# Keeping a convolution's output in DRAM instead of adding it up again from its two halves

## The chip, the cores and the metric

The kernel runs on one core of one Trainium2 chip, as one program in one launch. The metric is the device time of an execution in microseconds (us). Where a profile is shown, it comes from one profiled execution; its span runs from the first to the last instruction. The engines are called by the profile's names: PE is TensorE (PEld its weight loads), DVE is VectorE, ACT is ScalarE, POOL is GpSimd, and SP is the sequencer that issues most DMAs.

## The reference

One inference step of a small two-layer decoder trunk, all in float32: 1024 prompt tokens and 8 sequences of 4 sample tokens, 1056 columns together, model width 1024. The first layer is a gated linear recurrence (RG-LRU) of width 1536, the second one is HGRN2. Only the first is touched here:

```python
def _causal_conv(xb, w, b, buf):
    T = xb.shape[1]
    xp = jnp.concatenate([buf.astype(xb.dtype), xb], axis=1)
    out = b
    for k in range(CONV_W):
        out = out + w[k] * xp[:, k:k + T]
    return out, xp[:, -(CONV_W - 1):]

def _rg_lru(xc, w_r, b_r, w_i, b_i, lam, h0):
    ...
    r = jax.nn.sigmoid(jnp.einsum('btni,nij->btnj', xh, w_r.astype(jnp.float32)).reshape(Bsz, T, W) + b_r)
    ig = jax.nn.sigmoid(jnp.einsum('btni,nij->btnj', xh, w_i.astype(jnp.float32)).reshape(Bsz, T, W) + b_i)
    log_a = -LRU_C * jax.nn.softplus(-lam.astype(jnp.float32)) * r
    a = jnp.exp(log_a)
    bterm = jnp.sqrt(-jnp.expm1(2.0 * log_a)) * (ig * xf)
    bterm = bterm.at[:, 0].add(a[:, 0] * h0.astype(jnp.float32))
    _, h = lax.associative_scan(_lru_combine, (a, bterm), axis=1)
    return h, h[:, -1]

def _lru_layer(x, g_norm, w_in, conv_w, conv_b, w_r, b_r, w_i, b_i, lam, w_out, h0, buf):
    xn = _rmsnorm(x, g_norm)
    u = xn @ w_in
    xb, gate = u[..., :W_LRU], u[..., W_LRU:]
    xc, new_buf = _causal_conv(xb, conv_w, conv_b, buf)
    h, h_last = _rg_lru(xc, w_r, b_r, w_i, b_i, lam, h0)
    y = (h * jax.nn.silu(gate.astype(jnp.float32))).astype(x.dtype)
    return x + y @ w_out, h_last.astype(x.dtype), new_buf.astype(x.dtype)
```

The convolution's output `xc` (in `_rg_lru` also `xf` and `xh`) is used three times: in the two gate products, and as the factor of `ig` in the recurrence's input.

## The kernel before

**Layout.** Features lie on the 128 partitions, tokens along the columns. The 1056 columns are worked in three chunks of 352 (`CH`, `NCH`). The 1536 features of the recurrence are 12 tiles `m` of 128, in four groups `g` of three tiles `j`.

**Products.** A float32 product is made of three matmuls (`mm3`, L245 to L249): both operands are split into a high and a low part of a shorter type, and high x high, high x low and low x high are summed in PSUM. `weights` (L378) loads a weight tile in pieces of 512 columns into a ring of three raw buffers, casts the high part on ACT and subtracts the low part on POOL or DVE into rings of four pieces each. `product` (L401) then runs 8 blocks of 128 rows, 24 matmuls of 352 columns, into one of four PSUM banks.

**The convolution** (`conv`, L474). For a tile and a chunk, the product is copied into `xb`, ACT starts `t` with the last tap (L508), and DVE adds three taps (L511). `t` is a buffer of a ring of three (`ts`), cut out of the tile `k`. Then a DMA copies 32 of its rows to `ST` (L514), ACT writes the high part of `t` (L516) and DVE the low part (L517) into `X`, the operands of the gate products.

**The recurrence** (`lru`, L549). For a group and a chunk: gate products from `X` (L573) and from `ST` (L579), Tanh on ACT, DMAs that put 32 rows of each result in place (`R<-td`, L585), then for each tile `j` the recurrence's input: POOL adds the two parts of `X` into a buffer `x` (L594, a ring of two, `xrs`, also cut out of `k`), DVE multiplies it with the gate (L595), and further DVE instructions and a scan (L615) follow.

**The order of the work.** Every operation is first recorded by `Flow.add` with its engine, an estimated duration, what it reads and writes, and a priority. `Flow.plan` (L104) lays the operations out on five engines (SP's queue is one of them, a DMA counts as an SP operation with a transfer time behind it), `Flow.back` derives new priorities from the end backwards, eight times, and for the first layer `Flow.search` (L171) tries 3000 random changes of the priorities in its first 60 us. The resulting order is what each engine gets. The estimate for POOL instructions marked `both` also holds back DVE instructions marked so (L123). The order of the big products on PE is fixed in the code (`main=True`): for the first layer, groups of gate and convolution tiles with `lru(g)` and the output products `out(g)` woven in (L908 to L930). Each engine runs its list in order; SP runs its DMA issues in order too, and each waits for its own semaphores.

At the start, 48 matmuls on a constant tile (L739) are recorded with the lowest priority and fill what PE has free.

The helpers that record one operation:

```python
        def dma(dst, src, r=(), w=(), prio=5, kb=180, q=Q):
            fl.add("SP" if q is Q else "ACT", 0.45, lambda: q.dma_start(dst, src), r, w, prio, kb * (1.0 if r else 0.75))
...
        def pool(n, emit, r, w, prio=5):
            fl.add("POOL", 0.1 + 0.00245 * n, emit, r, w, prio, both=True)
...
        ks = [(KR[:, chunk(i)], ("k", i)) for i in range(KB)]
        ts, xrs = cycle(ks[:3]), cycle(ks[3:])
```

Of the kernel before, what the change touches and what calls it, by code (L numbers as in the profile page):

```python
# [14 lines left out]
F32 = mybir.dt.float32  # L15
# [4 lines left out]
ALU = mybir.AluOpType  # L20
# [21 lines left out]
TOK = SEQ + NB * NS  # L42
CH = 352
# [3 lines left out]
ML = WL // 128  # L47
# [168 lines left out]
def tile_trunk(ctx: ExitStack, tc: tile.TileContext, xT, prm, hc, w0, wg, wo0, w1, wo1, s_in,  # L216
               yT, h_out, c_out, sp_out, ss_out):
    nc = tc.nc
    V, S, G, T, Q = nc.vector, nc.scalar, nc.gpsimd, nc.tensor, nc.sync
# [15 lines left out]
    def pc(name, j, n=1):  # L235
        a = PRM[name][0] + j
        return P[:, a:a + n]
# [4 lines left out]
    def chunk(c):  # L242
        return slice(c * CH, (c + 1) * CH)
# [26 lines left out]
    x1a = [nc.dram_tensor(f"x1a_{m}", (128, TOK), F32, kind="Internal").ap() for m in range(KD)]  # L270
    x1d = [nc.dram_tensor(f"x1_{m}", (128, TOK), F32, kind="Internal").ap() for m in range(KD)]

    xn = nc.dram_tensor("xn", (KD, 128, TOK), F32, kind="Internal").ap()

    KR = chunks.tile([128, KB * CH], F32, tag="k", bufs=1, name="k")
# [27 lines left out]
    with ExitStack() as l0:  # L303
# [12 lines left out]
        def dma(dst, src, r=(), w=(), prio=5, kb=180, q=Q):  # L316
            fl.add("SP" if q is Q else "ACT", 0.45, lambda: q.dma_start(dst, src), r, w, prio, kb * (1.0 if r else 0.75))
# [6 lines left out]
        def act(n, emit, r, w, prio=5, more=0.0):  # L324
            fl.add("ACT", 0.25 + 0.0007 * n + more, emit, r, w, prio)

        def dve(n, emit, r, w, prio=5, both=False):
            fl.add("DVE", 0.13 + 0.0011 * n, emit, r, w, prio, both=both)

        def pool(n, emit, r, w, prio=5):  # L330
            fl.add("POOL", 0.1 + 0.00245 * n, emit, r, w, prio, both=True)
# [41 lines left out]
        def xpart(j, i, c):  # L373

            b = 6 * c + 2 * j + i
            return X[:, b * CH:(b + 1) * CH], ("X", b)
# [97 lines left out]
        def conv(g, head=False):  # L474

            items = []
            for j in range(3):
                m = 3 * g + j
                mine = {}

                def evac(c, ps, pk, by=None, j=j, m=m, mine=mine):
                    n = CH if c < 2 else 1024 - 2 * CH
                    if c == 0:
                        mine[0] = next(xbs)
                        pool(3, lambda xb=mine[0][0]: G.memset(xb[:, :3], 0.0), (), (mine[0][1],), 2)
                    elif head:
                        mine[c] = next(xbs)
                        pool(3, lambda xb=mine[c][0]: G.tensor_copy(xb[:, :3], tails[:, 4 * j:4 * j + 3]), (("tail", j),), (mine[c][1],), 0)
                    xb, xk = mine[c]
                    t, tk = next(ts)  # L490
                    if by:
                        dve(n, lambda: V.tensor_tensor(xb[:, 3:3 + n], ps[:, :n], by[0], op=ALU.mult), (pk, by[1]), (xk,), 0)
                        pool(3, lambda: G.tensor_copy(tails[:, 4 * j:4 * j + 3], xb[:, n:n + 3]), (xk,), (("tail", j),), 1)
                    else:
                        act(n, lambda: S.copy(xb[:, 3:3 + n], ps[:, :n]), (pk,), (xk,), 0)
                    if c < 2 and not by:
                        nx, nk = mine[c + 1] = (tails[:, 4 * j:], ("tail", j)) if head else next(xbs)
                        act(3, lambda: S.copy(nx[:, :3], ps[:, CH - 3:CH]), (pk,), (nk,), 0)
                    parts = [(xb[:, :3 + n], t[:, :n], lambda ap, i: ap[:, i:i + n], n)]
                    if c == 2:  # L500
                        xs = xb[:, 323:379].rearrange("p (b j) -> p b j", j=7)
                        pool(24, lambda: G.tensor_copy(xs[:, :, :3], cs[:, m]), (("hct",),), (xk,), 1)
                        act(32, lambda: S.copy(xs[:, :, 3:], ps[:, n:CH].rearrange("p (b j) -> p b j", j=4)), (pk,), (xk,), 0)
                        pool(3, lambda: G.tensor_copy(cst[:, m, 0, :], xb[:, 320:323]), (xk,), (("cst", m),), 4)
                        pool(24, lambda: G.tensor_copy(cst[:, m, 1:, :], xs[:, :, 4:7]), (xk,), (("cst", m, 1),), 4)
                        parts.append((xs, t[:, n:].rearrange("p (b j) -> p b j", j=4), lambda ap, i: ap[:, :, i:i + 4], 32))
                    for src, dst, sh, u in parts:
                        act(u, lambda src=src, dst=dst, sh=sh: S.activation(dst, sh(src, 3), AF.Identity, bias=pc("cb", m),  # L508
                                                                         scale=pc("cw", 36 + m)), (xk, ("P",)), (tk,), 1, 0.1)
                        for k in range(3):  # L510
                            dve(u, lambda src=src, dst=dst, sh=sh, k=k: V.scalar_tensor_tensor(  # L511
                                dst, sh(src, k), pc("cw", 12 * k + m), dst, op0=ALU.mult, op1=ALU.add), (xk, tk), (tk,), 1, True)
                    w = slice(32 * j, 32 * j + 32)
                    dma(ST[w, chunk(c)], t[w], (tk,), (("ST", j, c),), 1, 45)  # L514
                    (a, ak), (b, bk) = xpart(j, 0, c), xpart(j, 1, c)
                    act(CH, lambda: S.copy(a, t), (tk,), (ak,), 1)  # L516
                    dve(CH, lambda: V.tensor_tensor(b, t, a.bitcast(F32), op=ALU.subtract), (tk, ak), (bk,), 1, True)  # L517

                items.append((w0[m], evac))
            return items  # L520

# [27 lines left out]
        def lru(g):  # L549
# [11 lines left out]
            for c in range(NCH):  # L561
# [5 lines left out]
                for i, hb in ((0, hbr), (1, hbi)):  # L567
                    for j in range(3):
                        m = 3 * g + j
# [16 lines left out]
                for j in range(3):  # L586
                    m = 3 * g + j
                    act(CH, lambda j=j, m=m, ta=ta, ab=ab: S.activation(ab[:, j], ta[:, j], AF.Exp, bias=cn[:, m:m + 1], scale=cn[:, m:m + 1]),
                        (tak[j], ("sm",)), (("a", s, j),), 3, 0.15)
                    act(CH, lambda j=j, m=m, ta=ta: S.activation(ta[:, j], ta[:, j], AF.Tanh, bias=cp[:, m:m + 1], scale=cp[:, m:m + 1]),  # L590
                        (tak[j], ("sm",)), (tak[j],), 3, 0.15)
                    x, xk = next(xrs)
                    (a, ak), (b, bk) = xpart(j, 0, c), xpart(j, 1, c)
                    pool(CH, lambda x=x, a=a, b=b: G.tensor_tensor(x, a.bitcast(F32), b.bitcast(F32), op=ALU.add), (ak, bk), (xk,), 3)  # L594
                    dve(CH, lambda x=x, j=j, ti=ti: V.scalar_tensor_tensor(ti[:, j], ti[:, j], 1.0, x, op0=ALU.add, op1=ALU.mult),  # L595
                        (xk, tik[j]), (tik[j],), 3, True)

# [4 lines left out]
                for j in range(3):  # L602
                    m = 3 * g + j
# [302 lines left out]
        ysum = nc.dram_tensor("ysum", (3, 128, 8, HT), F32, kind="Internal").ap()  # L906
        x1b = [nc.dram_tensor(f"x1b_{m}", (128, TOK), F32, kind="Internal").ap() for m in range(KD)]
        lru(0)  # L908
        split_y(0)
        run(project0(gate(1)))  # L910
        run(project0(conv(1)))
        gates, rest = project0(gate(2)), out(0, xT, x1a)
        run(islice(gates, 6))
        lru(1)
        run(gates)
        run(project0(conv(2)))
        lru(2)
        run(rest)
        split_y(1)
# [19 lines left out]
    with ExitStack() as l1:  # L939
# [59 lines left out]
        def ykeys(m, a, n):  # L999

            return [("Y", m, i) for i, (u, v) in enumerate(zip(CUTS, CUTS[1:])) if u < a + n and v > a]
# [805 lines left out]
        for a, n in OUT:  # L1807
# [3 lines left out]
            acc, ak = next(accs)  # L1811
            tot, tk = next(hg)
            own = 4 if final else PS
            for m in range(KD):
# [12 lines left out]
                x, xk = x2[m][:, q], ykeys(Y2 + m, a, n)  # L1827
# [84 lines left out]
```

## Time and profile before

| | |
|---|---|
| median of the runs | 1056.82 us |
| lowest run | 1049.51 us |
| the profiled execution | 1050.79 us |
| its span | 1049.0 us |
| granted clock of TensorE, mean | 0.996 |
| HBM read / written | 81.60 / 33.05 MB |

Busy times in the page are shares of the span on each engine. Matmuls overlap: the next one starts before the last one has ended, so the time from start to start tells more than the length of one. "Idle before" of a group is the time that its engine stood still just ahead of it, with the instruction or DMA that ended the wait.

### The profile page before, as it was taken

Reading aid. Unit: us, or ns where it says so; the run is one execution under the profiler, and the core shown is the slowest. Engines: PE = TensorE matmul, PEld = TensorE weight load, DVE = VectorE, ACT = ScalarE, POOL = GpSimd, SP = SyncE. Lnnn points to the kernel's source line nnn. Section 1 sums busy time; section 2 is a strip of 40 time slices with the busy share of each in tenths; the row PEclk is TensorE's granted clock in tenths of the full one; section 3 lists DMA queues with packets and bytes.
Section 4 is the critical chain, followed back from the end, with each engine's and each line's share of the span. In section 5 each row is a group of like instructions: output and inputs, shape, how many; then the busy total and the mean of one; then the engine's idle time right before and its main releaser. Section 6 shows DMA issues by size and latency. Waiting matters only on the chain.

```text
span 1049.0 us, 26022 instructions
## 1 busy us (share of the span) xinstructions
PE 1029.1 (98%) x10174; PEld 1006.9 (96%) x10174; DVE 762.1 (73%) x1474; ACT 677.1 (65%) x1534; POOL 501.2 (48%) x526
## 2 busy tenths in 40 slices
PE   9999999999999999999999999999899999999995
PEld 9999999999999999999999999999899999999994
DVE  8999996788898689355687655555657567898648
ACT  6578656877775765334378685857577675785453
POOL 3425443544534355644655555555455453145454
PEclk9999999999999999999999999999999999999998
DMA  9101112123751586445676575655567662764644
GB/s 309 58 23 52 54 51 71 48 71 96 224 188 52 165 267 188 151 121 183 208 193 146 120 173 113 151 117 151 112 148 178 150 169 76 251 151 113 128 91 165
DMA packets 90763, 143.69 MB, mean 137 GB/s; under 512 B 11152, under 2 KB 56592, under 8 KB 90640
## 3 DMA queue, kind: packets, MB, share of 16 engines
q1 hardware_dynamic: 74656, 112.46, 34.0%
q0 software_dynamic: 13680, 26.81, 15.1%
q10 hardware_dynamic: 2304, 2.77, 0.8%
q8 instruction: 79, 1.29, 0.5%
q14 instruction: 44, 0.36, 0.1%
HBM read 81.60 MB, written 33.05 MB: 109 GB/s over the span
## 4 chain that ended last, share of the span: by engine, by line
PE 88%; DVE 8%; DMA 3%; issue 1%; ACT 0%; SPq 0%; ACTq 0%; DVEq 0%
PE mm L247 25%; PE mm L248 24%; PE mm L249 24%; PE hg L1063 2%; PE hg L1281 1%; PE hg L579 1%; PE hg L1174 1%; PE hg L1283 1%; PE hg L247 1%; PE hg L248 1%; PE hg L249 1%; DVE R L1045 1%; PE hg L1235 1%; DMA a<-in_w_dram 1%; DMA wraw<-in_wo_dram 1%; DVE R L445 1%
## 5 line engine op out<-in xcount | busy, mean ns | idle before, releaser
L247 PE MATMUL mm<-xh,whi 128*128 128x352 f32 (+1 forms) x1147 | 353.9, 309 | 5.0 <-DVE sg L1543 4.2
L248 PE MATMUL mm<-xl,whi 128*128 128x352 f32 (+1 forms) x1147 | 348.5, 304 | 0.0
L249 PE MATMUL mm<-xh,wlo 128*128 128x352 f32 (+1 forms) x1147 | 348.3, 304 | 0.0
L247 PEld LDWEIGHTS mm<-xh,whi 128*128 128x128 f32 x1147 | 215.5, 188 | 7.9 <-DVE sg L1543 4.8
L248 PEld LDWEIGHTS mm<-xl,whi 128*128 128x128 f32 x1147 | 215.6, 188 | 1.4
L249 PEld LDWEIGHTS mm<-xh,wlo 128*128 128x128 f32 x1147 | 215.6, 188 | 0.0
L335 POOL TENSOR_TENSOR wlo<-wraw,whi 128x512 fp32r<-128x512 f32 (+1 forms) x62 | 90.2, 1463 | 82.6 <-ACT whi L390 73.5
L247 PE MATMUL mm<-t,whi 128*128 128x264 f32 x408 | 118.3, 290 | 0.0
L249 PE MATMUL mm<-t,wlo 128*128 128x264 f32 x408 | 115.9, 284 | 0.7 <-POOL wlo L335 0.7
L248 PE MATMUL mm<-t,whi 128*128 128x264 f32 x408 | 115.7, 284 | 0.0
L511 DVE SCALAR_TENSOR_TENSOR k<-xb,prm_sb,k 128x352 f32<-128x352 f32 (+2 forms) x144 | 90.1, 637 | 10.9 <-ACT k L508 7.7
L247 PEld LDWEIGHTS mm<-t,whi 128*128 128x128 f32 x408 | 76.8, 188 | 0.9
L249 PEld LDWEIGHTS mm<-t,wlo 128*128 128x128 f32 x408 | 76.6, 188 | 0.9 <-POOL wlo L335 0.9
L248 PEld LDWEIGHTS mm<-t,whi 128*128 128x128 f32 x408 | 76.9, 188 | 0.1
L322 POOL DMA_DIRECT2D wlo<-wraw x52 | 45.4, 874 | 65.0 <-ACT wlo L321 45.9
L1543 DVE TENSOR_TENSOR k<-mm,k 128x264 f32<-128x264 f32 x72 | 30.8, 430 | 59.6 <-PE mm L249 56.4
L594 POOL TENSOR_TENSOR k<-X 128x352 f32<-128x352 f32 x36 | 43.8, 1226 | 48.0 <-DVE R L595 38.4
L322 POOL DMA_DIRECT2D wlo<-R x32 | 29.3, 923 | 44.7 <-ACT wlo L321 39.6
L247 PE MATMUL mm<-yh,whi 128*128 128x352 f32 x153 | 49.9, 326 | 0.0
L390 ACT CAST whi<-wraw 128x512 fp32r<-128x512 f32 (+1 forms) x63 | 36.3, 591 | 20.5 <-DMA wraw<-in_w_dram 10.1
L249 PE MATMUL mm<-yh,wlo 128*128 128x352 f32 x153 | 49.4, 323 | 0.0
L248 PE MATMUL mm<-yl,whi 128*128 128x352 f32 x153 | 49.4, 323 | 0.0
(423 smaller groups left out, 2688.7 us busy)
## 6 DMA issues: line engine op xcount, KB each, us to landing
wraw<-in_w_dram SPq DMA_DIRECT2D x88, 256.0 KB, 3.4
wlo<-wraw POOLq DMA_DIRECT2D x49, 256.0 KB, 4.2
wlo<-R POOLq DMA_DIRECT2D x30, 256.0 KB, 4.2
wraw<-in_wo_dram SPq DMA_DIRECT2D x37, 192.0 KB, 2.8
ysum<-sg SPq DMA_DIRECT2D x9, 528.0 KB, 5.2
si<-in_s_in_dram SPq DMA_DIRECT2D x8, 512.0 KB, 4.1
R<-in_w_dram SPq DMA_DIRECT2D x16, 256.0 KB, 3.6
out_ss_out_dram<-si SPq DMA_DIRECT2D x8, 512.0 KB, 2.9
```

What stands on the lines that cost most here:

```text
L247: T.matmul(out, wh, xh, start=first, stop=False, skip_group_check=chained)
L248: T.matmul(out, wh, xl, start=False, stop=False, skip_group_check=chained)
L249: T.matmul(out, wl, xh, start=False, stop=last, skip_group_check=chained)
L322: fl.add("POOL", 0.93, lambda: G.dma_start(dst.bitcast(F32), src, accum_op=ALU.add), (*r, *w), w, prio, n / 2)
L335: emit = lambda: e.tensor_tensor(b, x, a.bitcast(F32), op=ALU.subtract)
L390: act(m, lambda hi=hi, raw=raw, m=m: S.copy(hi[:, :m], raw[:, :m]), rk, (hk,), prio)
L445: (pool if e is G else dve)(CH, lambda: e.tensor_tensor(a[:, :CH], a[:, :CH], sq, op=ALU.add), (sk, ak), (ak,), 2)
L511: dve(u, lambda src=src, dst=dst, sh=sh, k=k: V.scalar_tensor_tensor(dst, sh(src, k), pc("cw", 12 * k + m), dst, op0=ALU.mult, op1=ALU.add ...
L579: fl.add("PE", 0.62, lambda ps=ps, i=i, c=c: T.matmul(ps[:96, :CH], gs[:, i, :], ST[:96, chunk(c)], start=True, stop=True), (("gs",), *((" ...
L594: pool(CH, lambda x=x, a=a, b=b: G.tensor_tensor(x, a.bitcast(F32), b.bitcast(F32), op=ALU.add), (ak, bk), (xk,), 3)
L1063: T.matmul(ps[32 * j:32 * j + 32, n * w:n * w + w], B[:, o:o + 32], q(slice(o, o + 32)), start=True, stop=True, tile_position=(0, 32 * j))
L1543: dve(QT, lambda: V.tensor_tensor(o[0], z[0], u[0], op=ALU.add), (z[1], u[1]), (o[1],), 0)
```

## The change

`conv` additionally stores the whole of `t` (128 rows, 352 columns) to a new DRAM tensor `tx`, right behind the small DMA to `ST`. `lru` loads this tile back into `x` with a DMA, where POOL added the two parts of `X`. Both DMAs are issued by SP. The value that the recurrence multiplies is then `t` itself. The same happens for all 12 tiles and three chunks.

```diff
@@ -270,6 +270,7 @@
     x1d = [nc.dram_tensor(f"x1_{m}", (128, TOK), F32, kind="Internal").ap() for m in range(KD)]
 
+    tx = nc.dram_tensor("tx", (ML, 128, TOK), F32, kind="Internal").ap()
     xn = nc.dram_tensor("xn", (KD, 128, TOK), F32, kind="Internal").ap()
@@ -512,6 +513,7 @@
                     w = slice(32 * j, 32 * j + 32)
                     dma(ST[w, chunk(c)], t[w], (tk,), (("ST", j, c),), 1, 45)
+                    dma(tx[m][:, chunk(c)], t, (tk,), (("tx", m, c),), 1)
                     (a, ak), (b, bk) = xpart(j, 0, c), xpart(j, 1, c)
@@ -590,8 +592,7 @@
                     x, xk = next(xrs)
-                    (a, ak), (b, bk) = xpart(j, 0, c), xpart(j, 1, c)
-                    pool(CH, lambda x=x, a=a, b=b: G.tensor_tensor(x, a.bitcast(F32), b.bitcast(F32), op=ALU.add), (ak, bk), (xk,), 3)
+                    dma(x, tx[m][:, chunk(c)], (("tx", m, c),), (xk,), 3)
                     dve(CH, lambda x=x, j=j, ti=ti: V.scalar_tensor_tensor(ti[:, j], ti[:, j], 1.0, x, op0=ALU.add, op1=ALU.mult),
                         (xk, tik[j]), (tik[j],), 3, True)
```

## The prediction

> **What bounds the kernel now.** I read the page's head first, then where the busy time of each engine lies by stage, then who TensorE waited for, and last the matmuls one by one. The page:
>
> ```profile
> span 1049.0 us, 26022 instructions
> PE 1029.1 (98%) x10174; PEld 1006.9 (96%) x10174; DVE 762.1 (73%) x1474; ACT 677.1 (65%) x1534; POOL 501.2 (48%) x526
> PE 88%; DVE 8%; DMA 3%; issue 1%; ACT 0%; SPq 0%; ACTq 0%; DVEq 0%
> ```
>
> TensorE is busy for 98% of the span and makes 88% of the chain that ended last; GpSimd, which the change relieves, is not in that chain's list at all. A share of busy time is an average, so the next view cuts the span into stages (columns: length, then busy time and instructions of each engine, granted clock, DMA share, GB/s):
>
> ```profile
> 0.00:18.00 18.00, 16.96 (x118) 16.96 (x119) 13.32 (x33) 12.58 (x26) 5.72 (x13) 1.00 0.91 314
> 18.00:44.00 26.00, 25.90 (x161) 24.95 (x161) 25.20 (x53) 16.43 (x35) 12.90 (x13) 1.00 0.44 138
> 44.00:534.00 490.00, 490.00 (x3101) 482.80 (x3102) 382.14 (x674) 304.60 (x594) 230.37 (x256) 1.00 0.40 123
> 534.00:944.00 410.00, 404.01 (x6078) 394.26 (x6067) 267.88 (x567) 293.77 (x751) 202.56 (x193) 1.00 0.62 150
> 944.00:1049.00 105.00, 92.22 (x744) 87.92 (x742) 73.51 (x152) 49.77 (x130) 49.59 (x53) 0.96 0.49 124
> ```
>
> The third row is the first layer after its start: 490.00 us of TensorE in 490.00 us. All of TensorE's idle time, 1049.0 - 1029.1 = 20 us, lies in the other rows, and nearly all of it behind 534 us, in the second layer and the tail, which the diff doesn't touch. The waits of TensorE, whole kernel (us in all, times, longest):
>
> ```profile
> PE mm L247 <- DVE sg L1543: 4.2, 3, 2.9
> PE hg L740 <- DVE ones L259: 1.0, 1, 1.0
> PE mm L1226 <- issue: 0.8, 1, 0.8
> PE mm L247 <- DVE vst L1190: 0.8, 1, 0.8
> PE mm L249 <- POOL wlo L335: 0.7, 1, 0.7
> PE mm L1226 <- DVE R L1697: 0.5, 1, 0.5
> PE hg L1149 <- DVE sg L1045: 0.4, 1, 0.4
> ```
>
> No row names a line of the first layer's recurrence (L549 to L625) as what TensorE waited for. Matmuls overlap, so "busy" could still hide bubbles; their starts tell:
>
> ```profile
> 120.05 0.32 PE L247 MATMUL mm<-xh,whi 128*128 128x352 f32 x1
> 120.21 0.32 PE L248 MATMUL mm<-xl,whi 128*128 128x352 f32 x1
> 120.37 0.32 PE L249 MATMUL mm<-xh,wlo 128*128 128x352 f32 x1
> ```
>
> One starts every 0.16 us, although each lasts 0.32; 490.00 / 3101 = 0.158 us for the stage as a whole is the same pace. The stage is a closed row of matmuls at a granted clock of 1.00. The change removes no matmul, so this stage can't become shorter than 490 us.
>
> [...]
>
> **The change part by part.** The removed and the neighbouring work, from the lines' own answers (count, then minimum/median/maximum in ns, first and last start in us), and from the groups:
>
> ```profile
> L594 POOL TENSOR_TENSOR k<-X x36: 934/1171/2000, 85.8 to 394.5; 128x352 f32<-128x352 f32 x36
> L594 POOL TENSOR_TENSOR k<-X 128x352 f32<-128x352 f32 x36 | 43.8, 1226 | 48.0 <-DVE R L595 38.4 <-DVE X L517 7.3 <-DVE nr L452 1.9
> L595 DVE SCALAR_TENSOR_TENSOR R<-R,k x36: 509/524/1622, 87.8 to 395.5; 128x352 f32<-128x352 f32 x36
> L595 DVE SCALAR_TENSOR_TENSOR R<-R,k 128x352 f32<-128x352 f32 x36 | 28.9, 820 | 10.1 <-DMA R<-td 8.0 <-POOL k L594 2.1
> L317 SPq DMA_DIRECT2D ST<-k x36: 507/512/1707, 48.6 to 355.8; - x36
> ```
>
> (1) Removed: 36 additions on GpSimd, 36 x 1.226 = 43.8 us of its 230.37 us in the stage. GpSimd had 490.00 - 230.37 = 260 us to spare there; TensorE waited for none of the 36. Worth 0 us on the path. Vector waited 2.1 us for them in all, also beside TensorE.
>
> (2) Relief of VectorE: L595 takes 509 ns at best and 820 ns on average, so something stretches it by 36 x 0.31 = 11 us. GpSimd runs beside it, and with 36 GpSimd instructions gone part of that goes. VectorE has 382.14 of 490.00 us, so the 11 us (at most the 43.8 us that GpSimd gives up) fall into its own slack of 108 us: 0 us on the path.
>
> [...]
>
> (3) Added: 36 stores and 36 loads of 128 x 352 x 4 bytes = 176 KB. No row has exactly these, but stores and loads of the same tiles and size to and from DRAM are there (KB, us from issue to landing):
>
> ```profile
> ST<-k SPq DMA_DIRECT2D x36, 44.0 KB, 1.8
> x1a<-k SPq DMA_DIRECT2D x9, 176.0 KB, 3.2
> k<-x1a SPq DMA_DIRECT2D x9, 176.0 KB, 3.8
> wraw<-in_w_dram SPq DMA_DIRECT2D x88, 256.0 KB, 3.4
> ```
>
> A tile thus takes 3.2 + 3.8 = 7.0 us through DRAM, where the addition took 1.2. It has far longer: the small store of the same `t` (ST<-k) runs from 48.6 to 355.8 us and the additions from 85.8 to 394.5, so the first value is wanted 37 us, and the last 39 us, after it exists. The latency costs 0 us. Were a load late all the same, L595 would wait, and behind it on VectorE the taps and the copies that empty TensorE's banks. Traffic: 72 x 180,224 bytes = 13.0 MB; at the 314 GB/s of the first row of stages (DMA share 0.91) that is 41 us of full DMA, spread over about 350 us in a stage with a share of 0.40. It becomes about 0.5. The crowded place is the end of the layer:
>
> ```profile
> 346.00:396.00 50.00, 50.00 (x304) 48.54 (x303) 36.96 (x61) 38.86 (x66) 26.29 (x21) 1.00 0.75 229
> ```
>
> There some 9 loads and a few stores join, 12 x 0.18 MB / 314 GB/s = 7 us into 50 us that have 12 us free. It fits, by little.
>
> (4) SP's queue: 72 issues more, at the 0.51 us of the small store's row 37 us of sequencer time. All of SP's issues stand in order, so what counts is who is held behind a waiting one. The store follows the small store of the same tile and waits for the same VectorE instruction, so it adds no wait. The load waits for its buffer `x` (two of them), that is for the L595 of two tiles before, and behind it stand weight loads. SP's queue already does such waiting:
>
> ```profile
> SPq L317 <- DVE k L511: 65.2, 22, 14.9
> SPq L317 <- POOL wlo L335: 64.7, 32, 10.0
> ```
>
> (Between 44 and 434 us.) It stood up to 14.9 us behind a convolution tile without TensorE noticing. The cover is the ring of four weight pieces: a piece of 512 columns feeds 4 blocks x 3 chunks x 3 matmuls x 0.16 = 5.8 us, so the two pieces ahead feed 11.5 us. The nearest row for the new wait is the addition's wait for the same buffer, today on GpSimd's queue:
>
> ```profile
> POOL k L594 <- DVE R L595: 38.4, 14, 8.1
> ```
>
> So the ends are 0 and 38.4 us, for holds of at most 8.1. As 8.1 is under the cover of 11.5, I take 0.
>
> (5) `t` is held until the larger store has landed, 3.2 instead of 1.8 us, plus 0.5 us of issue: 1.9 us longer in a ring of three. ScalarE's next write of `t` would queue behind it, then the release of the product's PSUM bank. A product takes 24 x 0.16 = 3.8 us and there are four banks, so 1.9 us stay covered.
>
> (6) The order of the whole first layer is planned again with the new costs, and the random search over its first 60 us draws differently. Where this shows is the start, in which idle matmuls fill the holes between real ones:
>
> ```profile
> 10.31 0.41 PE L247 MATMUL mm<-xh,whi 128*128 128x352 f32 x1
> 11.34 2.17 PE L740 MATMUL hg<-ones 128*128 128x128 f32 x18
> 15.46 1.27 PE L740 MATMUL hg<-ones 128*128 128x128 f32 x10
> 17.06 0.61 PE L740 MATMUL hg<-ones 128*128 128x128 f32 x4
> ```
>
> From 10.31 to about 17.4 us the fillers take about 4 us (2.17 + 1.27 + 0.61, and short groups between). A better start can gain these 4 us at most; a worse one may lose as much. I take 0.
>
> Sum: 0 us against the profiled execution's 1050.79 us (span 1049.0 and 1.8 us around it). The median of the runs shown is 1056.82 with a lowest of 1049.51, so the profiled one is near the low end. Forecast: **1051 us**, and 6 us of spread between runs above it.
>
> **The rivals.**
> *Covered, no change* (chance 0.84): 1047 to 1057 us, by (6) and the spread.
> *The end of the layer crowds* (0.08): the 7 us of traffic in 346 to 396 us meet a share of 0.75 and weights come late by what doesn't fit: 1051 + 7 = 1058, to 1062 with a worse start. For it: 0.75. Against: no wait of TensorE there today.
> *SP's queue holds the weights* (0.06), the case on the slow side: a load that waits for `x` stands ahead of weight loads. It decides once a hold outlasts the 11.5 us of weights ahead; each us beyond is one of TensorE's. If the ring gives no cover, all of 38.4 us come through: 1089 us; half of it, 1070, would still be within 2%. Against: 14.9 us of hold are survived now, and the addition's longest wait was 8.1.
> *VectorE was the bound after all* (0.02): then 11 us of stretch go, 1040 us, and in the extreme all 43.8 us, 1007 us. Against: the third stage row.
> That the change doesn't take the additions off GpSimd can be excluded: their only line is the one replaced.
>
> **How the numbers follow.** About 2% (21 us) is what a measurement of this kernel can tell from no change. Gains are bounded by 4 us of fillers (1047, and one for run to run: 1046), losses that keep 8 in 10 by the crowded end: 1062. The VectorE case splits, half of it over 2%: faster 0.01, and I give 0.02 for what I don't see; of the SP case half lies beyond 1072, 0.03, and 0.02 again for what I don't see: 0.05 slower; the rest, 0.93, is within.
>
> **What would show it.** In the profile after: no GpSimd line for the addition, GpSimd near 457 us busy in all, 72 DMAs more of 176 KB and 13 MB more traffic, L595's successor nearer 0.5 than 0.8 us, and the stretch from 44 to 534 us still full of TensorE with the same count of matmuls. The forecast is wrong if a row of TensorE's waits names a weight piece (`whi`, `wlo`) or a convolution's bank inside that stretch, or if the first dense matmul moves by several us from 17.4.

## The result, and the profile after

Nine runs of the changed kernel have a median of 1058.59 us (1055.69 to 1061.0), nine of the kernel before 1050.95 us; the ratio is 1.0079, with a 95% interval of 1.006 to 1.0098. The ratios here and below leave disturbed runs out (here one of the kernel before, 2045.15 us), so they can differ a little from the quotient of two medians. The change costs some 8 us (0.79%). That is inside the range of the prediction and far under 2%, but it isn't the "no change" that was forecast. The profiled execution took 1057.43 us, 6.64 more than that of before.

The head of the page after, and the two new groups of its list of DMA issues (KB each, us from issue to landing):

```profile
span 1055.7 us, 26100 instructions
PE 1034.6 (98%) x10174; PEld 1011.9 (96%) x10174; DVE 747.9 (71%) x1474; ACT 678.3 (64%) x1534; POOL 456.4 (43%) x490
tx<-k SPq DMA_DIRECT2D x36, 176.0 KB, 2.1
k<-tx SPq DMA_DIRECT2D x36, 176.0 KB, 2.7
```

GpSimd has lost 44.8 us (501.2 to 456.4), VectorE 14.2, and the chip takes longer. The stages (length, then busy time and instructions of PE, PEld, DVE, ACT, POOL, the granted clock, DMA share, GB/s):

```profile
18.00:44.00 26.00, 22.36 (x126) 21.34 (x125) 23.83 (x47) 15.92 (x34) 12.26 (x12) 0.87 0.49 157
44.00:534.00 490.00, 490.00 (x3065) 483.01 (x3065) 365.97 (x675) 301.05 (x586) 183.48 (x218) 1.00 0.47 145
```

In the second row TensorE is as full as before: 490.00 of 490.00. But it has 3065 matmuls in it, where there were 3101: the work has been pushed back by something ahead of it. The first row has 126 matmuls instead of 161, 3.5 us less busy time and a granted clock of 0.87 instead of 1.00. TensorE's longest waits (us in all, times, longest):

```profile
PE mm L247 <- DVE sg L541: 3.6, 1, 3.6
PE mm L247 <- DVE sg L1544: 2.4, 4, 0.9
```

The first row is new. L541 (L539 before) multiplies a gate product with the norm's scale on its way out of the bank; it is called the copy below. The second is L1543 of before, in the second layer; it had 4.2 us, longest 2.9. The place of the new wait in TensorE's timeline (start, us, engine, line):

```profile
31.43 0.32 PE L248 MATMUL mm<-xl,yh 128*128 128x352 f32 x1
31.59 0.32 PE L249 MATMUL mm<-xh,yl 128*128 128x352 f32 x1
35.55 0.66 PE L247 MATMUL mm<-xh,yh 128*128 128x352 f32 x1 [3.64 <-DVE sg L541]
36.01 0.49 PE L248 MATMUL mm<-xl,yh 128*128 128x352 f32 x1
36.30 0.49 PE L249 MATMUL mm<-xh,yl 128*128 128x352 f32 x1
36.60 0.49 PE L247 MATMUL mm<-xh,yh 128*128 128x352 f32 x1
```

Two things are to be seen. TensorE stands still for 3.64 us; and when it goes on, one matmul starts every 0.29 us instead of every 0.16. The clock in the two stretches:

```profile
31.70:35.50 3.80, 0.21 (x2) 0.00 (x0) 3.70 (x6) 0.83 (x3) 2.90 (x3) 0.80 0.28 73
35.50:41.00 5.50, 5.45 (x17) 4.94 (x18) 4.27 (x10) 3.52 (x8) 0.85 (x2) 0.52 0.48 161
```

A clock of half goes with the stop: in the trace's clock records it falls from 1.00 to 0.50 at 33.99 us and rises again at 40.81. When it fell, TensorE had stood idle for 2.1 us (its last matmul ended at 31.91 us). The last section comes back to this.

Why the bank was not emptied is seen on VectorE. After:

```profile
29.63 4.39 DVE L446 TENSOR_TENSOR R<-R,xo 128x352 f32<-128x352 f32 x4
33.94 0.94 DVE L461 TENSOR_TENSOR k<-ident,nr 128x256 f32<-128x256 f32 x1
34.81 0.26 DVE L464 TENSOR_SCALAR k<-ident,nr 128x96 f32<-128x96 f32 x1
34.99 1.37 DVE L541 TENSOR_TENSOR sg<-mm,R 128x352 f32<-128x352 f32 x3
```

and before:

```profile
29.75 1.15 DVE L445 TENSOR_TENSOR R<-R,xo 128x352 f32<-128x352 f32 x2
30.82 0.52 DVE L539 TENSOR_TENSOR sg<-mm,R 128x352 f32<-128x352 f32 x1
```

L446 (before L445) sums the squares of a later chunk's norm. At this place it was done twice, and then came the copies; now it is done four times, then a norm's scaling, and the copies come 4.2 us later (34.99 against 30.82). Four additions would take 2.3 us at the pace of the two (1.15). They take 4.39, and in that time GpSimd subtracts beside them (in the kernel before, two of them beside such a subtraction, from 27.34 us, took 2.07; that GpSimd is what stretches them was not tested):

```profile
30.83 1.31 POOL L336 TENSOR_TENSOR yl<-wraw,yh 128x512 fp32r<-128x512 f32 x1
32.09 2.51 POOL L559 TENSOR_TENSOR gl<-wraw,gh 128x512 fp32r<-128x512 f32 x2
```

None of these instructions was changed. They stand in another order.

How much later each matmul starts than before follows from comparing the n-th matmul of L247 in both traces (my own working from the starts): -0.1 us at n=31 (31.3 us), +3.7 at n=32, +6.1 at n=40, +5.7 at n=140 (88 us), +8.1 at n=700 and n=1000 (517 us), up to +9.2 in the second layer, +6.6 at the last one. So the 6.6 us of the two profiled executions are 3.7 of standstill, 2.4 of half clock (0.4 of it regained by 88 us), 2.4 of a slow drift from there to 517 us, 1.1 more in the second layer, and 2.6 that the second layer gives back (1.8 of it in its waits for L1543, now L1544, which go from 4.2 to 2.4).

The drift is a pace. Between 100 and 200 us, before and then after:

```profile
100.00:200.00 100.00, 100.00 (x616) 98.30 (x616) 83.08 (x141) 68.04 (x134) 39.55 (x44) 1.00 0.19 56
```

```profile
100.00:200.00 100.00, 100.00 (x612) 98.54 (x611) 78.49 (x142) 69.76 (x139) 29.18 (x41) 1.00 0.33 98
```

TensorE is full and at clock 1.00 in both, with four matmuls fewer. The mean from start to start of the matmuls of 352 columns and 128 rows between 100 and 520 us, holes left out (anything from 200 ns on), is 159.90 ns before and 160.88 after.

### The profile page after: what moved, and what is told of

It reads as the page before. It is cut to its first block, busy times and chain, and to the rows that moved or that the text cites. A ratio compares the mean times of both kernels' runs of the same rounds, so it can differ in the third digit from the quotient of the medians.

```text
span 1055.7 us, 26100 instructions
## 1 busy us (share of the span) xinstructions
PE 1034.6 (98%) x10174; PEld 1011.9 (96%) x10174; DVE 747.9 (71%) x1474; ACT 678.3 (64%) x1534; POOL 456.4 (43%) x490
## 2 busy tenths in 40 slices
DMA packets 101131, 156.68 MB, mean 148 GB/s; under 512 B 12304, under 2 KB 66960, under 8 KB 101008
## 4 chain that ended last, share of the span: by engine, by line
PE 90%; DVE 6%; DMA 2%; issue 1%; POOL 1%; ACT 0%; ACTq 0%; DVEq 0%; POOLq 0%
PE mm L247 25%; PE mm L249 25%; PE mm L248 25%; PE hg L1064 2%; PE hg L1175 1%; PE hg L1282 1%; PE hg L581 1%; PE hg L1284 1%; PE hg L249 1%; PE hg L247 1%; PE hg L248 1%; DMA wraw<-in_w_dram 1%; PE hg L1236 1%; DVE R L446 1%; PE hg L1326 1%; DMA sg<-xn 1%
## 5 line engine op out<-in xcount | busy, mean ns | idle before, releaser
L247 PE MATMUL mm<-xh,whi 128*128 128x352 f32 (+1 forms) x1147 | 354.5, 309 | 2.7 <-DVE sg L1544 2.4
L247 PEld LDWEIGHTS mm<-xh,whi 128*128 128x128 f32 x1147 | 215.8, 188 | 6.2 <-DVE sg L1544 3.2
L247 PE MATMUL mm<-t,whi 128*128 128x264 f32 x408 | 118.3, 290 | 0.0
L512 DVE SCALAR_TENSOR_TENSOR k<-xb,prm_sb,k 128x352 f32<-128x352 f32 (+2 forms) x144 | 84.9, 596 | 14.6 <-ACT k L509 8.3
L247 PEld LDWEIGHTS mm<-t,whi 128*128 128x128 f32 x408 | 76.8, 188 | 0.9
L323 POOL DMA_DIRECT2D wlo<-wraw x52 | 45.4, 874 | 65.0 <-ACT wlo L322 44.8
L1544 DVE TENSOR_TENSOR k<-mm,k 128x264 f32<-128x264 f32 x72 | 30.7, 429 | 58.6 <-PE mm L249 55.9
L247 PE MATMUL mm<-yh,whi 128*128 128x352 f32 x153 | 51.6, 337 | 0.0
L322 ACT ACTIVATE wlo<-wraw 128x512 fp32r<-128x512 f32 (+1 forms) x52 | 32.4, 623 | 21.1 <-PE mm L249 10.4
```

The costliest lines, as they stand in the source:

```text
L247: T.matmul(out, wh, xh, start=first, stop=False, skip_group_check=chained)
L322: act(n, lambda: S.activation(dst, src, AF.Copy, scale=-1.0), r, w, prio)
L323: fl.add("POOL", 0.93, lambda: G.dma_start(dst.bitcast(F32), src, accum_op=ALU.add), (*r, *w), w, prio, n / 2)
L1544: dve(QT, lambda: V.tensor_tensor(o[0], z[0], u[0], op=ALU.add), (z[1], u[1]), (o[1],), 0)
```

## The experiments

Two questions: is it the work that was exchanged (additions for transfers) or the order that the planner made of it? And what are the 6 us and the drift? "Pace" below is the mean start to start as above. The ratio is that against the kernel before on the same chip.

| run | order of the start | work | ratio, 95% | pace, ns |
|---|---|---|---|---|
| e1 | old | transfers | 1.0011 (0.9992 to 1.003) | 159.92 |
| e2 | new | additions | 1.0067 (1.0044 to 1.0091) | 160.89 |
| e3 | new, hole filled | transfers | 1.006 (1.0038 to 1.0082) | 160.88 |
| e5 | new, copies earlier | transfers | 1.0051 (1.0031 to 1.0071) | 160.88 |
| e9 | old, new behind 46 us | transfers | 1.0001 (0.9987 to 1.0015) | 159.99 |
| e10 | new, old behind 46 us | transfers | 1.0067 (1.005 to 1.0083) | 160.87 |
| e7 | old | transfers twice | 1.0069 (1.0046 to 1.0093) | 159.89 |
| e6 | old, one idle matmul | additions | 0.9997 (0.9987 to 1.0008) | 159.90 |
| e15 | old, 17 idle matmuls | additions | 1.0019 (1.0002 to 1.0036) | 159.91 |
| e4, e11 | other draws | additions | 1.0048 (1.0028 to 1.0069), 1.0028 (1.0009 to 1.0048) | 160.75, 160.81 |
| e8, e12 | other draws | transfers | 1.009 (1.006 to 1.012), 1.0084 (1.0055 to 1.0114) | 160.92, 160.88 |
| e13 | no search | additions | 1.0035 (1.0017 to 1.0054) | 160.49 |
| e14 | no search | transfers | 1.0044 (1.0022 to 1.0065) | 160.44 |

**Work and order apart (e1, e2).** Both lists of operations are recorded. One is planned as its kernel plans it; the starts of that plan are given to the other list as priorities, which so gets the first one's order. An operation that only the issued list has is put where its counterpart stood: a store behind the small store of its tile, a load 3 us ahead of the addition, an addition where the load was. e1:

```diff
-            fl.run(SEARCH, 60.0)
+            _, _, at = fl.planned("old", SEARCH, 60.0)
...
+            plan, ids = fl.flow("new")
...
+            plan.best = plan.plan([at[n] for n in ids])
+            plan.issue(plan.best[3])
```

e2 has "old" and "new" exchanged.

> The changed kernel's work (36 stores, 36 loads, no additions on GpSimd), but laid out with the priorities of the kernel before, so that its start (up to the first store, about 48 us) is instruction for instruction that of the kernel before. Theory A (the loss is the start: a new order of the first 44 us, which the planner drew when the list of operations changed): the 32nd triple of matmuls starts near 31.8 us instead of 35.6, no hole of TensorE, granted clock 1.00 before 44 us, 1050 to 1053 us. Theory B (the loss is the 13 MB of transfers, or their place in the queue): 1056 to 1060 us although the start is the old one. In between, 1052 to 1054 us with matmuls at 161.0 ns from start to start instead of 160.05, if the transfers cost the slow drift of 2.4 us alone.

> The other way round: the additions on GpSimd and no store or load, laid out with the priorities of the changed kernel, so that the start is that of the changed kernel. Theory A: the hole of about 4 us near 31.6 us and the clock at half behind it are there, and 1056 to 1060 us. Theory B: 1049 to 1052 us. If the drift of 2.4 us belongs to the transfers: 1055 to 1057 us, matmuls at 160.0 ns.

Measured: e1 1049.02 us against 1048.71, e2 1056.48. In the stages, e1 first (18 to 44 us and the first layer), then e2 (18 to 44 us):

```profile
18.00:44.00 26.00, 25.52 (x159) 24.43 (x158) 25.20 (x53) 17.07 (x36) 13.10 (x14) 1.00 0.46 158
44.00:534.00 490.00, 490.00 (x3081) 483.02 (x3080) 363.23 (x674) 303.84 (x593) 182.91 (x221) 1.00 0.48 149
```

```profile
18.00:44.00 26.00, 21.28 (x114) 19.98 (x114) 23.52 (x48) 16.46 (x35) 11.67 (x12) 0.87 0.52 163
```

e1 makes all 72 transfers and none of the additions (POOL 182.91, DVE 363.23 us), and it is as fast as the kernel before. e2 makes no transfer, and it has the low clock, the hole (a wait of 4.1 us for the copy, behind the matmul of 31.45 us) and the pace of the changed kernel. The order carries the loss; the work carries none that these runs can tell (by e1's interval at most 0.3%).

**Which part of the order (e9, e10).** As e1, with the starts of two plans joined at 46 us: what one list's plan starts before 46 us keeps its place, everything else goes by the other's. e9 has the old start, e10 the new one; both make the transfers.

```diff
+            for n, start in one.items():
+                if start < 46.0:
+                    at[n] = start
+                elif n in at:
+                    at[n] = max(at[n], 46.0)
```

> The changed kernel's work, with the old priorities for everything that the planner began before 46 us and the new ones behind it. It parts the loss of the start (5.7 us) from the slow drift behind it (2.4 us to the end of the first layer). If the drift belongs to the start (whatever the half clock or the hole sets going): matmuls every 159.9 ns, no drift, 1048 to 1050 us. If it belongs to the order of the rest of the layer: no hole, offset under 1 us at the 60th triple, then 160.8 ns and a drift of 2 to 3 us by the 1000th, 1050 to 1052 us.

> The other half: the new priorities up to 46 us, the old ones behind, with the transfers. The hole and 6 us of offset at the 60th triple under both. If the drift belongs to the start: 160.8 ns and 1056 to 1059 us. If it belongs to the order of the rest: 159.9 ns, the offset stays at 6 us through the layer, 1053 to 1056 us.

Measured: 1048.85 and 1055.59 us against 1048.56. The start of e9, then of e10:

```profile
18.00:44.00 26.00, 24.69 (x152) 23.50 (x152) 25.20 (x53) 17.01 (x36) 13.08 (x14) 1.00 0.47 149
```

```profile
18.00:44.00 26.00, 22.64 (x126) 21.64 (x125) 23.73 (x47) 15.72 (x34) 12.20 (x12) 0.87 0.49 158
```

All of the loss goes with the first 46 us, the drift included, although it happens behind them.

**The half clock (e3).** The changed kernel, with 17 idle matmuls on a constant tile (into a bank that nobody reads) in the hole, so that TensorE doesn't stand still there.

```diff
+            plan.filler = 32, 17, lambda: T.matmul(warm[:, :128], ones, ones, start=True, stop=True)
             plan.issue(plan.best[3])
```

> The changed kernel in its own order, with 17 idle matmuls on a constant tile (3.6 us) put into the hole, behind the 32nd triple of TensorE. They can't shorten the wait for the bank. Theory A with the clock as a part of the price: the granted clock stays at 1.00, the matmuls behind the hole start every 160 ns instead of 293, the offset to the kernel before at the 40th triple is 3.7 us instead of 6.1, and the time falls by about 2.4 us against the changed kernel, to 1055 or 1056 us. If the clock falls for another reason than the idle TensorE, or its fall costs nothing: no change, 1058 to 1059 us.

Measured: 1055.06 us against 1048.71. The stretch of the hole and the one behind it:

```profile
31.00:35.50 4.50, 4.46 (x39) 4.27 (x37) 4.30 (x5) 1.76 (x5) 3.82 (x4) 1.00 0.21 54
35.50:41.00 5.50, 5.23 (x31) 5.02 (x32) 5.50 (x13) 4.62 (x10) 1.37 (x2) 1.00 0.47 167
```

The clock stays at 1.00, and the matmul n=40 is 3.9 us late instead of 6.1. So some 2.2 us of the loss at this place are the half clock, and the rest is the standstill itself. The drift stays (pace 160.88), so it isn't a matter of the clock having fallen.

**The copies moved up (e5).** The three copies of L541, with the ScalarE copy that they need, are put in the issued order right behind what they depend on.

```diff
+            for what in (("bcs", 0, 0), ("evac", 0, 0), ("evac", 1, 0), ("evac", 2, 0)):
+                i = mine[what]
+                at = order.index(i)
+                to = max(order.index(d) for d in plan.ops[i][3]) + 1
+                order.insert(to, order.pop(at))
```

> The changed kernel in its own order, with four instructions moved: ScalarE's copy of the first chunk's norm ahead of one weight cast, and VectorE's three instructions that empty the first three product banks ahead of two additions of squares and the norm's two scalings. If the hole comes from these three standing too late on VectorE, they start near 31.5 us instead of 35.0, the hole of 4 us and the half clock go, the offset to the kernel before at the 40th triple is 0 to 3 us instead of 6.1, and the time is 1050 to 1054 us. If the hole has another cause (weights, or the second chunk's norm, which is now later), it moves by a few us and the time stays at 1056 to 1059 us.

Measured: 1054.13 us against 1048.92. The copies now start at 31.68 us, and what stands behind them is late instead (in this kernel's lines L291 to L293 are the three matmuls, L585 is the copy, L508 the norm's scaling):

```profile
31.42 0.32 PE L293 MATMUL mm<-xh,yl 128*128 128x352 f32 x1
33.12 0.43 PE L291 MATMUL mm<-xh,yh 128*128 128x352 f32 x1 [1.38 <-DVE sg L585]
...
34.02 0.32 PE L293 MATMUL mm<-xh,yl 128*128 128x352 f32 x1
35.61 1.54 PE L510 MATMUL hg<-k,ones 128*128 128x352 f32 x2 [1.26 <-DVE k L508]
```

One hole of 4 us has become two of 1.7 and 1.6 (33.12 - 31.42 and 35.61 - 34.02), and the clock falls all the same: 0.50 between 35.5 and 41 us. At n=40 it is 5.6 us late. By these rows VectorE has too much due between 29 and 36 us in this order; moving one piece up makes the next one late.

**The transfers doubled (e7).** In the old order, each tile is stored to a second tensor too, and loaded from both: 144 DMAs and 26 MB in place of 72 and 13. It tests the prediction's items (3) to (5) with twice their price.

```diff
+                    fl.mark(("new", "store2", m, c), lambda: dma(ty[m][:, chunk(c)], t, (tk,), (("ty", m, c),), 1))
...
+                    fl.mark(("new", "load", m, c), lambda x=x, m=m, c=c: dma(x, ty[m][:, chunk(c)], (("ty", m, c),), (xk,), 3))
```

> The first experiment of this case again (the changed kernel's work in the old order) with every store and load done twice, to and from a second tensor: 144 DMAs and 26 MB more than the kernel before. Theory A: the stage behind 44 us is still a closed row of matmuls, and the time is within 2 us of the once-only version, 1048 to 1051 us. If the transfers are near their limit, waits of TensorE for weights appear between 250 and 400 us, where the DMA share was already 0.75, and the time is 1055 us or more.

Measured: 1056.67 us against 1048.92. The start is as before (n=40: +0.2 us), the pace too. The time is lost in the layer: waits of TensorE between 44 and 534 us, and the stretch from 340 to 400 us, after that the same stretch in e1:

```profile
PE hg L291 <- ACT R L623: 1.9, 1, 1.9
PE mm L291 <- DVE xo L696: 1.8, 2, 1.1
PE mm L291 <- DVE k L582: 0.5, 1, 0.5
340.00:400.00 60.00, 57.31 (x336) 55.27 (x335) 39.59 (x71) 42.56 (x79) 15.92 (x15) 0.97 0.79 252
```

```profile
340.00:400.00 60.00, 60.00 (x366) 58.55 (x365) 42.66 (x78) 46.02 (x84) 16.75 (x15) 1.00 0.76 239
```

With one store and one load a tile the layer stays full; with two it has four holes, and 2.7 of their 4.2 us lie where the prediction looked for them, at the crowded end. None of them is a wait for a weight piece: TensorE waits for a gate's Tanh on ACT (L623) and for banks that VectorE empties late. The reserve is real, and it is smaller than a second helping. Which of the doubled prices (bandwidth, SP's queue, the longer hold of `t`) is the first to come through was not separated.

**The random draws (e4, e8, e11, e12).** The kernels before and after, with another seed for the search in `Flow.search`: 2 (e4, e8) and 3 (e11, e12). The last argument is the seed; this is e4, the others differ in it and in "old" or "new".

```diff
-            fl.run(SEARCH, 60.0)
+            plan, ids, _ = fl.planned("old", SEARCH, 60.0, 2)
```

> The kernel before with nothing changed but the seed of the planner's random search (2 instead of 1). The planner gives this order the same end as the old one. Theory A says that the start is a draw that the planner can't tell apart: the offset of the matmuls at the 60th triple differs from that of the kernel before by anything between 0 and some 6 us either way, and so does the time, 1047 to 1058 us. Theory B: 1050 to 1052 us, within 1 us of the kernel before.

> The changed kernel with nothing but the seed of the planner's search changed (2 instead of 1). Theory A: another draw of the start; the loss at the 60th triple is somewhere between 0 and 6 us, and the time between 1048 and 1058 us, not tied to the 1057 of the first draw. Theory B: 1056 to 1060 us again.

> The kernel before with a third seed of the planner's search. If the start of the kernel before is a draw like any other, this one lies on either side of it, 1045 to 1056 us. If it is one of the better draws, as the second seed's ratio of 1.0048 suggests, this one is slower again, 1051 to 1058 us, and its matmuls start every 160.7 to 160.9 ns.

> The changed kernel with a third seed. The transfers cost nothing in the old order, so its time should scatter like that of the kernel before under other seeds: 1051 to 1059 us. A time at or below 1049 us would be a version of the change that is not slower without borrowing the old order.

Measured, in this order: 1053.99, 1056.17, 1051.34 and 1059.06 us. The kernel before loses 3 and 5 us by nothing but another draw, so its start is itself a good draw. The changed list is at +0.8 to +0.9% in all three of its draws, so its loss isn't one bad draw either.

**Without the search (e13, e14).** `SEARCH` replaced by 0; the order is that of the backward priorities.

```diff
-            fl.run(SEARCH, 60.0)
+            plan, ids, _ = fl.planned("old", 0, 60.0)
```

> The kernel before with its random search left out: the order is that of the backward priorities alone. Theory A (the random search is what makes the one start good and the other bad): this start has holes of its own, the time is 4 to 10 us above the kernel before, like that of the changed list without search. Theory B (the priorities that the search starts from differ, since 36 GpSimd operations are gone and 72 transfers are there): within 3 us of the kernel before, and the changed list without search is 5 us or more above it. In both the matmuls of 100 to 520 us start every 160.7 to 160.9 ns unless the start is the old one, as in all other starts so far.

> The changed kernel with its random search left out. Theory A (search): within 2 us of the kernel before without search. Theory B (priorities): 5 us or more above the kernel before without search, with a wait of TensorE for a gate product's evacuation near 31 us, as in the changed kernel.

Measured: 1052.45 and 1052.51 us against 1048.70. The start of e13, then of e14:

```profile
18.00:44.00 26.00, 24.24 (x150) 23.23 (x149) 24.99 (x49) 17.17 (x38) 13.06 (x13) 1.00 0.49 159
```

```profile
18.00:44.00 26.00, 24.15 (x142) 23.18 (x141) 24.64 (x48) 16.64 (x35) 12.51 (x13) 0.93 0.49 159
```

Without the search the two lists are equally fast as far as these runs can tell (+0.35% and +0.44%, with intervals that overlap): it is the search that parts them, although e14's start has a hole of its own and a granted clock of 0.93. With the seed as it is, the search takes 0.35% off the kernel before and adds as much to the changed one (0.79% instead of 0.44%). In the plan itself this isn't seen: the end of the layer that the planner reckons with is 507.60 us for all six searched starts, and 507.78 (e13) and 508.02 us (e14) for the two without (the planner's own arithmetic, no time of the chip). `Flow.search` keeps a change of the priorities when its aim is no later than before (`<=`), so among starts that the plan holds equal it wanders. That the three draws on the changed list are all worse than no search, while those on the list before lie around it (0, +0.5, +0.3% against +0.35%), may have a reason or be chance; six draws don't settle it.

**The pace (e6, e15).** The kernel before in its own order, with one idle matmul behind its second triple of matmuls (e6), and with 17 at the place where the changed kernel has its hole (e15). Neither alters a result.

```diff
+            plan.filler = 32, 17, lambda: T.matmul(warm[:, :128], ones, ones, start=True, stop=True)
```

(e6: 2, 1 instead of 32, 17.)

> The kernel before in its own order, with one more idle matmul of 0.2 us behind the second triple of TensorE, where TensorE is waiting anyway. It disputes the slow drift: in the runs so far the matmuls of the first layer start every 159.9 ns in two kernels that share the old start and every 160.8 to 160.9 ns in the other four, with the transfers and without. If the drift hangs on where the matmuls stand in the instruction stream, one instruction more may bring it: 160.8 ns, offset growing from 0 to 2 or 3 us over the layer, 1050 to 1052 us. If it hangs on VectorE's and ScalarE's order or on the hole, it stays at 159.9 ns and the time at 1048 to 1050 us.

> The kernel before in its own order, with 17 idle matmuls (about 4 us of TensorE, into a bank that nobody reads) at the place where the changed kernel's hole is, near 31.5 us: only the moment moves at which everything behind stands, not the order. Theory C (the slower pace of the matmuls behind the start comes from the later moment: something with a clock of its own): the matmuls of 100 to 520 us start every 160.7 to 160.9 ns, and the time is 6 to 7 us above the kernel before. Theory D (it comes from the order of the start, not from its length): 159.9 ns, and about 4 us above, less what fits into waits of the second layer.

Measured: e6 1048.97 us against 1048.92, e15 1050.92 against 1048.70, which is half of the 4 us that were reckoned for the idle matmuls. In e15 the matmuls behind the start stand 2.35 us later from n=60 to n=1000, without any drift between:

```profile
100.00:200.00 100.00, 100.00 (x618) 98.54 (x617) 82.91 (x143) 67.89 (x135) 40.45 (x50) 1.00 0.19 55
```

So the pace belongs neither to one instruction more nor to the later moment, but to the order of the start. In the kernel before, 19 matmuls between 100 and 520 us come 166 ns or more after the one ahead of them; after, 208. They aren't tied to a companion: taken only where GpSimd is idle, or ScalarE, or VectorE, the products of the input weights still have about 160 ns before and 161 after. By what an order of the first 46 us slows matmuls 100 to 400 us later stays open.

## Why the prediction was right or wrong

**Items (1) and (2), 36 additions and VectorE's relief at 0 us: right.** GpSimd came to 456.4 us (forecast 457). The multiplication that follows went from 820 to 654 ns, in the first layer's groups (busy us, mean ns, then idle before and its releasers):

```profile
L596 DVE SCALAR_TENSOR_TENSOR R<-R,k 128x352 f32<-128x352 f32 x36 | 23.4, 654 | 9.8 <-DMA R<-td 5.5 <-ACT a L590 2.2 <-DMA k<-tx 1.8
```

That is nearer to 0.5 than to 0.8, by little: half of the stretch remains. In e1, where the mean is 572 ns, all of this relief buys no time.

**Item (3), the transfers at 0 us: right.** 156.68 MB moved instead of 143.69, so 13.0; 2.1 and 2.7 us a tile, less than the 3.2 and 3.8 of the nearest rows; the share of the DMA engines in the stage 0.47 (forecast 0.5), and in the 50 us of the crowded end 0.74, with TensorE busy for all 50. The row of L596 shows 1.8 us in which VectorE waited for the loads. e7 shows that the place was rightly called crowded, though TensorE's waits there were not for weights.

**Items (4) and (5), SP's queue and the longer hold of `t`: right.** No wait of TensorE between 44 and 534 us, for a weight piece or anything else; in e1 the stage is as full.

**Item (6), the new order of the start at 0 us, is the step that failed.** It saw that the whole start is planned again and that the search draws differently, and it then took the 4 us of fillers between 10 and 17 us for the most that a better start can gain and for what a worse one "may lose as much". The gain is bounded by idle time that is there. The loss isn't: a worse order makes new idle time, 3.7 us at a place (31.6 us) that was full before, then 2.2 to 2.4 us of half clock behind it, then a pace that is 0.6% slower for 400 us (2.4 us; why, stays open). And "I take 0" took the middle of a draw that wasn't centred: the start of the kernel before is the best of its three seeds and 3.8 us better than no search, so a new draw was likely to be worse. The forecast needed a term of its own for it. By these runs another draw, or none, costs 0.3 to 0.9%, 3 to 9 us, against the kernel before (e4, e8, e11 to e14). The forecast's "6 us of spread" came from a median of three runs; of the nine of the kernel before, seven lie between 1047.67 and 1051.18.

**The check named for it was the right one, at the wrong place.** That "the first dense matmul moves by several us from 17.4" was to show the forecast wrong. The matmuls up to 31.3 us have not moved (-0.1 us); the start came apart behind that. The sign that did show it was the count: 3065 matmuls between 44 and 534 us, where the forecast wanted the same 3101.

**The rivals.** The crowded end and SP's queue cost nothing here. The band of "covered, no change" (1047 to 1057) misses the median by 1.6 us; the range reached it only through the price of another mechanism, the crowded end, so that is luck.

## What to carry to other kernels

Where an order is planned or searched anew after every edit, the edit is two changes, and they are measured apart: issue the new work in the old order first (e1), and draw the old kernel's order again (e4, e11, e13) to learn how good a draw it had. A start that is a good draw is likely lost by any edit that draws again (here 3 and 5 us in the kernel before itself, e11 and e4), so forecast that loss as a term of its own, with a price. A search that keeps equals of a plan wanders among orders that the chip doesn't hold equal (here six starts of 507.60 us in the plan, 1049 to 1059 us measured); where the plan can't tell them apart, keep the order that was measured.

## What the hardware showed that I had not expected

A standstill of TensorE can be paid one and a half times (after, 3.7 us of it brought 2.4 us of half clock), and its length alone doesn't say whether it is. The longest wait of the second layer took 2.9 us in the kernel before (its row stands in the prediction) and 3.2 in e1 (whose L1606 is L1543 of before):

```profile
PE mm L291 <- DVE sg L1606: 5.2, 5, 3.2
```

In the clock records of the kernel before, of the changed one and of e1 the changes lie at multiples of 3.413 us from the first rise: before, the clock rises at 6.88 and falls at 1041.12 (303 pieces later); after, it rises at 6.68, falls at 33.99 (8 pieces later) and rises at 40.81 (2 pieces); in e1 it rises at 7.28, falls at 758.21 (220 pieces) and rises at 761.63 (1 piece). Cut into these pieces, the two waits look different (columns as in the stages above, idle time is the length less PE's busy time); before, then e1:

```profile
750.98:754.40 3.42, 2.04 (x17) 1.83 (x15) 3.17 (x7) 0.49 (x1) 3.27 (x5) 1.00 0.43 77
754.40:757.81 3.41, 1.89 (x15) 1.89 (x16) 3.37 (x8) 1.83 (x4) 1.27 (x2) 1.00 0.07 19
757.81:761.22 3.41, 3.41 (x30) 3.41 (x29) 2.02 (x6) 2.27 (x5) 1.06 (x2) 1.00 0.47 82
```

```profile
754.80:758.21 3.41, 0.37 (x3) 0.37 (x4) 3.37 (x5) 0.73 (x2) 2.09 (x2) 1.00 0.02 3
758.21:761.63 3.42, 3.42 (x18) 3.42 (x17) 2.45 (x8) 1.53 (x4) 0.89 (x1) 0.50 0.44 83
```

The 2.9 us lie across two pieces, 1.4 and 1.5 us idle in each, and the clock stays. The 3.2 us of e1 lie nearly whole in one piece (3.0 us idle), and the next piece goes at half; it costs e1's profiled execution 1.5 us in the second layer, in which no line was changed. Nor need it be one hole: in e5 the piece from 31.47 to 34.89 us has 1.9 us idle from two holes, and the clock falls at its end; in e14 it falls behind a piece with 1.85 us idle. The most idle time in a piece without a fall was 1.7 us (e6). One fall doesn't fit (e8, at 30.44 us, behind a piece with 1.2 us idle). This is read from the traces of these runs; no run was made to test it.

Matmuls in a closed row at full clock don't have one pace. The same 352 columns take 159.9 to 160.9 ns from start to start, for hundreds of microseconds, by the order of instructions in the first 46 us (e9 and e10); over the first layer that is 2 to 3 us, as much as the half clock. The cause is not known.
